# Sums of weight blocks formed in device memory for a seven-product multiply, with the products reordered

## The chip, the core and the metric

The kernel runs on one core of a Trainium2 chip. A core has five engines with an instruction queue each, worked off in order: TensorE (PE: matrix products and transposes, with the weight loads in a row of their own, PEld), VectorE (DVE), ScalarE (ACT), GpSimd (POOL) and SyncE (SP, which here only issues transfers). Engines wait for each other by semaphores. Transfers (DMAs) issued by SP or ACT ("hardware" queues, q1 and q10 in the profile) and by POOL ("software" queue, q0) run on the same 16 DMA engines. Operands of the engines lie in on-chip memory (SBUF), results of PE in accumulator banks (PSUM); weights and inputs lie in device memory (DRAM).

The metric is the device time of one execution in microseconds (us). Before the change: 1409.25 us, the median of 3 runs (1408.93 to 1411.69).

## What is computed

One layer of a hybrid block on 512 tokens of width 1024, everything in float32: a gated delta-rule branch "a" (8 heads) and a retention branch "b" (4 heads), both fed from one projection by `w_in`, gated, projected and mixed, then an MLP. Cut to what matters here:

```python
proj = xn @ w_in                       # 512 x 1024 times 1024 x 14352
qa, ka, va, za, ..., qb, kb, vb, gb, gate_a, gate_b = split(proj)
oa = chunk_gated_delta_rule(conv_silu(qa, ka, va), beta, g)
ya = (rmsnorm(oa) * silu(za)) @ w_br_a
ob = chunk_retention(rotary(qb), rotary(kb), vb)          # vb, gb: 4 heads x 512 columns
yb = (rmsnorm(ob) * silu(gb)) @ w_br_b
mix = (sigmoid(gate_a) * ya + sigmoid(gate_b) * yb) @ w_out
x = x + rmsnorm(mix)
out = x + rmsnorm(square(relu(rmsnorm(x) @ w_up)) @ w_down)
```

The change concerns `vb` and `gb`, the values and the gates of branch b: per head a product of the 512 x 1024 activations with two blocks of 1024 x 512 of `w_in`.

## The kernel before, in words

Every large product is made of three float32r products: operands are split into a high and a low part, and high x high, high x low and low x high are added in PSUM (`mm3`, L78, whose three matmuls are L81, L82 and L83). A weight block of 512 KB is loaded by SP into a tile `raw` (`weights`, L85, the load is on L91), then split: ACT copies the high part `whi` (L104), DVE subtracts to get the low part `wlo` (L105). Pool `ring` holds 2 `raw`, 3 `whi` and 3 `wlo`. A list `raw_pools` says from which pools `weights` takes `raw` in turn: the ring alone, and late in branch b also a tag `ych` with 2 buffers in the pool of that stage (`raw_pools.append`).

Stages in order of time:

- The input is normed, transposed and split into `xs` (tiles `actT`).
- Branch a (pools `pa` and, inside it, `pa2`): `keys`, `base_inverse`, `double_blocks`, `values_queries` and `recurrence` for four groups `g2` of two heads, then for each group `gated` (gate product), `ya_partial` of the group before, and `gated_features` (the group's result transposed, 4 times 4 transposes by PE on L202 through one PSUM bank, each four taken out by ACT on L185 and DVE on L186). In `values_queries` each of six convolutions (`conv_silu`, L378) first has POOL clear three columns of a tile `c_raw` with 2 buffers (L380), ACT fills the rest, DVE runs the taps (L390, L394) and PE transposes the result (`to_tokens`). POOL also masks `at` (`affine_select`, L588) and moves small blocks through DRAM scratch (`scr`, `rn`, `rt`).
- Branch b (pool `pb`, whose tiles take the memory that `pa2` and `pa` leave): `feature_sums` (sums of quarters of the activations, DVE and ACT), then for each head `h`: `scores` (products for q and k, `rotary` on DVE (L824 to L832), score products in PSUM tag `dl`), at h = 0 `ya_partial(3)` and the gate product of branch a, else `branch_partial`; `outputs`, with `values_and_gates` in it, and `gated_features`.
- Mixing, the output product and the MLP.

`values_and_gates` (L738) makes the values and gates of a head by a seven-product scheme (Strassen-Winograd) on 2 x 2 blocks: token halves by row halves of `w_in`, and the two column blocks c1 (values) and c2 (gates). Call the weight blocks w11, w12, w21, w22 (first index the row half, second c1 or c2). Four of the products need sums of weight blocks: w11+w12, w22+w12, w11+w12+w22, and all four. Each product takes two weight tiles of 512 KB (`ks` = 0, 1) and each tile feeds 12 matmuls on L758. Before, these sums are formed in SBUF just in time: class `Sums` (L111) keeps one `raw` tile per `ks` for a running sum ("chain", in tag `ych`): after DVE has split it for one product, POOL issues a transfer that adds the next block onto it (`accum_op=ALU.add`, L124), and it is split again. The order of products is 11, 12, s1, s3, s2, s4, 22.

The instructions are ordered on each engine when the program is built: the tile framework schedules by priorities (`tc.high_priority`), and `tc.keep_in_program_order` pins the matmuls of a product. Waits between tiles are set by it too: a tile of `pb` waits until the last readers and writers of the memory it takes from `pa` and `pa2` are done; and DMAs issued by POOL go through eight semaphore lanes in turn, so that one waits for the eighth before it.

Of the kernel before, what the change touches and what calls it, by code (L numbers as in the profile page):

```python
# [60 lines left out]
def hybrid_block_kernel(ctx: ExitStack, tc: tile.TileContext, a: dict, out: bass.AP):  # L61
# [46 lines left out]
            lo[:, :n].rearrange("p (k c) -> p k c", k=nk),  # L108
        )

    class Sums:  # L111


        def __init__(self, pool, tag, blocks):
            self.raw = pool.tile([P, 1024], F32, tag=tag, name="raw", bufs=2)
            self.blocks, self.n = blocks, 0

        def next(self, more=1):
            for _ in range(more):
                src, k0, c0 = self.blocks[self.n]  # L120
                block = src[k0 * P : (k0 + 2) * P, c0 : c0 + 512].rearrange("(k p) c -> p k c", p=P)
                dst = self.raw.rearrange("p (k c) -> p k c", k=2)
                if self.n:
                    nc.gpsimd.dma_start(dst, block, accum_op=ALU.add)  # L124
                else:
                    nc.sync.dma_start(dst, block)
                self.n += 1
            return split_weights(self.raw, 1024, 2)

    def feature_major(src, xs, c0, ncols, kts, krow0=0):  # L130

# [296 lines left out]
    with tc.tile_pool(name="pa", bufs=1) as pa:  # L428
# [46 lines left out]
        def base_inverse(g4, pool):  # L475
# [32 lines left out]
                nc.gpsimd.dma_start(rt[bs, ns, bs], scr_t[b].rearrange("n (m c) -> m n c", m=32))  # L508
            return scr_r

        def double_blocks(pool, scr_r, m0):

            rn = pool.tile([P, 8, 64], F32, tag="qf", name="rn", bufs=2)
            nc.gpsimd.memset(rn, 0.0)
            for b in range(3):
                bs = slice(32 * b, 32 * b + 32)
                cs = slice(32 * (b % 2), 32 * (b % 2) + 32)
                nc.gpsimd.dma_start(
                    rn[bs, :, cs], scr_r[b, m0 % 16 : m0 % 16 + 8].rearrange("n (m c) -> m n c", m=32)
                )  # L520
# [24 lines left out]
            nc.vector.tensor_scalar(rn[hi, :, 0:32], p2[hi], -1.0, None, ALU.mult)  # L545
            lo, hi = slice(0, 64), slice(64, 128)
            p3 = bank(64)
            for n in range(8):
                nc.tensor.matmul(p3[hi, n, :], mt[lo, m0 + n, hi], rn[lo, n, :], start=True, stop=True)
            nc.vector.tensor_copy(y[hi], p3[hi])  # L550
            p4 = bank(64)
            for n in range(8):
                nc.tensor.matmul(p4[lo, n, :], y[hi, n, :], rt[hi, m0 + n, hi], start=True, stop=True)
            nc.vector.tensor_scalar(rt[lo, ns, hi], p4[lo], -1.0, None, ALU.mult)

        def values_queries(g2, pool):
# [16 lines left out]
            for hh in range(2):  # L573
# [9 lines left out]
                for c in range(4):  # L583
# [4 lines left out]
            nc.gpsimd.affine_select(  # L588
                at, at, pattern=[[0, 8], [1, P]], compare_op=ALU.is_ge, fill=0.0, base=0, channel_multiplier=-1
            )  # L590

            rq = pool.tile([P, 8], F32, tag="rq", name="rq", bufs=2)
            nc.vector.tensor_scalar(ssq, ssq, EPS, None, ALU.add)
# [81 lines left out]
        def gated(g2, rows, pool):  # L675
            pss = token_major(w_in, x_tile, OFF_ZA + g2 * 512, 8)
            zz = pool.tile([P, 4, T], F32, tag="zz", name="zz")
            gate_rows(pss, rows, lambda t: zz[:, t, :])

        with tc.tile_pool(name="pa2", bufs=1) as pa2:  # L680
            keys(0, pa2)
            scr = base_inverse(0, pa2)
            vq = values_queries(0, pa2)
            keys(1, pa2)
            double_blocks(pa2, scr, 0)
            og = None
            for g2 in range(4):
                rows = recurrence(g2, vq, pa2)
                if g2 == 0:
                    double_blocks(pa2, scr, 8)  # L690
                    scr = base_inverse(1, pa2)
                if g2 < 3:
                    vq = values_queries(g2 + 1, pa2)
                if g2 == 1:
                    double_blocks(pa2, scr, 16)
                    double_blocks(pa2, scr, 24)
                gated(g2, rows, pa2)
                if g2:
                    ya_partial(g2 - 1, og)
                og = gated_features(rows, lambda f: na[:, f % 2 : f % 2 + 1])  # L700
# [3 lines left out]
    with tc.tile_pool(name="pb", bufs=1) as pb_:  # L704
# [6 lines left out]
        def tmp(name):  # L711
            return pb_.tile([P, T], F32, tag="tm", name=name, bufs=8)
# [20 lines left out]
                nc.vector.tensor_tensor(s[:, 1], a, s[:, 0], ALU.subtract)  # L733
                quarters[f"s{i + 1}"] = [s[:, 0], s[:, 1]]

        feature_sums()

        def values_and_gates(c1, c2, g, out1, out2):  # L738

            def rows(kh, ks):  # L740
                return 4 * kh + 2 * ks

            chain = [
                Sums(pb_, "ych", [(w_in, rows(0, ks), c1), (w_in, rows(0, ks), c2),
                                  (w_in, rows(1, ks), c2), (w_in, rows(1, ks), c1)])
                for ks in range(2)
            ]

            def product(pss, x, ks, wts, first):
                wh, wl = wts  # L750
# [17 lines left out]
            def bank():  # L768
                return [psm.tile([P, T], F32, tag="mm", name="mm") for _ in range(2)]

            def one(kh, c, ks):
                return Sums(ring, "raw", [(w_in, rows(kh, ks), c)]).next()

            def two(ks):
                return Sums(ring, "raw", [(w_in, rows(1, ks), c2), (w_in, rows(0, ks), c2)]).next(2)

            a = bank()
            for ks in range(2):
                product(a, "11", ks, chain[ks].next(), True)
            p1 = [tmp("p1") for _ in range(2)]  # L780
            with tc.high_priority(400):
                for t in range(2):
                    nc.scalar.copy(p1[t], a[t])
            for ks in range(2):
                product(a, "12", ks, one(1, c1, ks), False)
            for t in range(2):
                out1(t, a[t])
            c = bank()
            for ks in range(2):
                product(c, "s1", ks, chain[ks].next(), True)  # L790
# [4 lines left out]
            for ks in range(2):  # L795
                product(b, "s3", ks, two(ks), True)
# [4 lines left out]
            for ks in range(2):  # L801
                product(b, "s2", ks, chain[ks].next(), False)
            u3s = [tmp("u3") for _ in range(2)]
            with tc.high_priority(400):
                for t in range(2):
                    nc.vector.tensor_tensor(u3s[t], p1[t], b[t], ALU.add)
            for t, u3 in enumerate(u3s):
                nc.vector.tensor_tensor(p7[t], u3, p7[t], ALU.subtract)
                nc.vector.tensor_tensor(g[:, 2 + t, :], g[:, 2 + t, :], u3, ALU.subtract)
                out2(2 + t)  # L810
            for ks in range(2):
                product(c, "s4", ks, one(1, c2, ks), False)
# [3 lines left out]
            for ks in range(2):  # L816
                product(b, "22", ks, chain[ks].next(), False)
            for t in range(2):
                nc.vector.tensor_tensor(p1[t], p1[t], b[t], ALU.add)
                out1(2 + t, p1[t])  # L820

        def rotary(pss, dst):
            r = [tmp("ro") for _ in range(4)]
# [39 lines left out]
        def outputs(h, scs):  # L863
# [13 lines left out]
            values_and_gates(OFF_VB + h * 512, OFF_GB + h * 512, gs, value, gate)  # L877
# [266 lines left out]
```

## Time and profile before

| what | value |
| --- | --- |
| median of three runs | 1409.25 us (1408.93 to 1411.69) |
| the profiled execution: its own time | 1408.78 us |
| its span in the trace | 1407.1 us |
| PEld busy | 1124.0 us (80%) |
| DVE, ACT, POOL busy | 869.7 us (62%), 611.2 us (43%), 93.4 us (7%) |
| mean granted TensorE clock | 0.993 |
| read from DRAM / written | 143.81 MB / 5.77 MB, 106 GB/s over the span |
| values and gates of the four heads (first and last start on L758) | 587.1 to 921.7 us |

The trace lists the instructions of one execution with their start, their duration and what ended the idle time before them. Matmuls are pipelined: one of 512 columns lasts 0.39 us in the records while the next starts 0.227 us after it, so that a gap under about 0.16 us doesn't show as idle PE; the weight loads (PEld) show it. "PEclk" is the clock granted to TensorE as a share of full speed. A view by windows gives the busy time of each engine in a stretch, the clock, the mean share of the 16 DMA engines and what they moved.

### The profile page before, as it was taken

The numbers are of one execution on the slowest core, as the hardware profiler recorded it, in microseconds if no ns is written. First come the engines' busy times: TensorE is split into PE (matmuls) and PEld (weight loads), VectorE is DVE, ScalarE is ACT, GpSimd is POOL, SyncE is SP. The second block draws the span as 40 slices with busy tenths as digits, with TensorE's granted clock in tenths as the row PEclk, the third lists the DMA queues.
The fourth block names the chain that finished last, engine by engine and source line by source line (L and its number), as shares of the span: only waits on it lengthen the run. The fifth ranks groups of instructions, "written<-read, shape, count | busy, mean of one in ns | idle before, by whom it ended". The sixth has DMA issues, their size and how long they took to land.

```text
span 1407.1 us, 17528 instructions
## 1 busy us (share of the span) xinstructions
PE 1377.1 (98%) x6670; PEld 1124.0 (80%) x6670; DVE 869.7 (62%) x1539; ACT 611.2 (43%) x1134; POOL 93.4 (7%) x136
## 2 busy tenths in 40 slices
PE   8999999999999989999999999999999999999997
PEld 5888787878888878877878778778888888888886
DVE  5599889944755594467378486565785334344445
ACT  6778564725534232343453443443354333232331
POOL 1112300200000000110200200200000000000000
PEclk9999999999999999999999999999999999999999
DMA  5232412221321333682672753851724232323321
GB/s 158 75 93 74 118 31 75 71 78 46 90 90 45 104 115 97 166 208 75 120 187 82 151 150 76 184 174 61 229 99 137 92 103 90 105 90 105 105 75 61
DMA packets 79223, 150.72 MB, mean 107 GB/s; under 512 B 5183, under 2 KB 18641, under 8 KB 78626
## 3 DMA queue, kind: packets, MB, share of 16 engines
q1 hardware_dynamic: 66128, 119.03, 27.4%
q0 software_dynamic: 12288, 29.32, 10.2%
q8 instruction: 52, 0.85, 0.2%
q10 hardware_dynamic: 722, 1.25, 0.2%
q14 instruction: 33, 0.27, 0.1%
HBM read 143.81 MB, written 5.77 MB: 106 GB/s over the span
## 4 chain that ended last, share of the span: by engine, by line
PE 79%; DVE 9%; DMA 6%; ACT 3%; issue 2%; POOL 0%; SPq 0%; DVEq 0%; POOLq 0%; ACTq 0%
PE mm L81 21%; PE mm L82 21%; PE mm L83 21%; DMA raw<-in_w_in_dram 5%; PE mm L758 4%; DVE wlo L105 3%; PE tr L202 2%; ACT whi L104 2%; DVE c_y L390 1%; PE dl L621 1%; PE dl L649 1%; PE dl L82 1%; PE dl L81 1%; PE dl L83 1%; PE dl L613 1%
## 5 line engine op out<-in xcount | busy, mean ns | idle before, releaser
L105 DVE TENSOR_TENSOR wlo<-raw,whi 128x1024 fp32r<-128x1024 f32 x232 | 283.6, 1223 | 357.3 <-ACT whi L104 356.0
L104 ACT CAST whi<-raw 128x1024 fp32r<-128x1024 f32 x232 | 243.9, 1052 | 473.4 <-PE mm L82 239.3
L82 PE MATMUL mm<-actT,whi 128*128 128x512 f32 (+1 forms) x528 | 209.2, 396 | 1.2 <-DVE actT L236 1.2
L81 PE MATMUL mm<-actT,whi 128*128 128x512 f32 (+1 forms) x528 | 206.5, 392 | 1.0 <-ACT actT L235 1.0
L83 PE MATMUL mm<-actT,wlo 128*128 128x512 f32 (+1 forms) x528 | 207.1, 393 | 0.0
L81 PEld LDWEIGHTS mm<-actT,whi 128*128 128x128 f32 x528 | 99.7, 189 | 21.6 <-ACT actT L235 1.4
L82 PEld LDWEIGHTS mm<-actT,whi 128*128 128x128 f32 x528 | 100.3, 190 | 20.3 <-DVE actT L236 1.4
L83 PEld LDWEIGHTS mm<-actT,wlo 128*128 128x128 f32 x528 | 100.1, 190 | 18.4
L81 PE MATMUL mm<-hn,whi 128*128 128x512 f32 (+1 forms) x288 | 105.6, 367 | 0.5 <-DVE r L1067 0.5
L82 PE MATMUL mm<-hn,whi 128*128 128x512 f32 (+1 forms) x288 | 105.4, 366 | 0.0
L81 PE MATMUL mm<-og,whi 128*128 128x512 f32 x256 | 100.9, 394 | 4.3 <-DVE ro L825 4.3
L83 PE MATMUL mm<-hn,wlo 128*128 128x512 f32 (+1 forms) x288 | 105.1, 366 | 0.0
L83 PE MATMUL mm<-og,wlo 128*128 128x512 f32 x256 | 100.6, 393 | 0.0
L82 PE MATMUL mm<-og,whi 128*128 128x512 f32 x256 | 100.6, 393 | 0.0
L81 PE MATMUL mm<-whi,actT 128*128 128x512 f32 x216 | 86.2, 399 | 0.1
L82 PE MATMUL mm<-wlo,actT 128*128 128x512 f32 x216 | 85.8, 397 | 0.0
L83 PE MATMUL mm<-whi,actT 128*128 128x512 f32 x216 | 85.5, 397 | 0.0
L758 PE MATMUL mm<-whi,xsum 128*128 128x512 f32 x256 | 82.3, 397 | 2.0 <-ACT whi L104 2.0
L390 DVE SCALAR_TENSOR_TENSOR c_y<-c_raw,convw,c_y 128x512 f32<-128x512 f32 x96 | 70.5, 752 | 3.4 <-ACT c_y L388 2.8
L81 PEld LDWEIGHTS mm<-hn,whi 128*128 128x128 f32 x288 | 54.3, 188 | 10.1 <-DVE r L1067 0.8
L83 PEld LDWEIGHTS mm<-hn,wlo 128*128 128x128 f32 x288 | 54.2, 189 | 8.8
L82 PEld LDWEIGHTS mm<-hn,whi 128*128 128x128 f32 x288 | 54.3, 189 | 8.7
(314 smaller groups left out, 2468.2 us busy)
## 6 DMA issues: line engine op xcount, KB each, us to landing
raw<-in_w_in_dram SPq DMA_DIRECT2D x113, 512.0 KB, 3.8
raw<-in_w_up_dram SPq DMA_DIRECT2D x36, 512.0 KB, 3.8
raw<-in_w_in_dram POOLq DMA_DIRECT2D x32, 512.0 KB, 7.0
raw<-in_w_down_dram SPq DMA_DIRECT2D x32, 512.0 KB, 3.7
raw<-in_w_br_a_dram SPq DMA_DIRECT2D x16, 512.0 KB, 3.7
raw<-in_w_br_b_dram SPq DMA_DIRECT2D x16, 512.0 KB, 3.7
raw<-in_w_out_dram SPq DMA_DIRECT2D x8, 512.0 KB, 3.9
x<-in_x_dram SPq DMA_DIRECT2D x4, 512.0 KB, 6.1
```

Of the source, the lines that this page charges most:

```text
L81: nc.tensor.matmul(ps, lh, rh, start=first, stop=False)
L82: nc.tensor.matmul(ps, lh, rl, start=False, stop=False)
L83: nc.tensor.matmul(ps, ll, rh, start=False, stop=last)
L104: nc.scalar.copy(hi[:, :n], raw[:, :n])
L105: nc.vector.tensor_tensor(lo[:, :n], raw[:, :n], hi[:, :n], ALU.subtract)
L202: nc.tensor.transpose(ps, src, ident)
L390: nc.vector.scalar_tensor_tensor(y, raw[:, j : j + T], tap(j), y, ALU.mult, ALU.add)
L613: nc.tensor.matmul(ks[:, hh, :], kf[:, h0 + hh, cs], state[:, hh, :], start=True, stop=True)
L621: nc.tensor.matmul(px[:, hh, :], rt[:, nn[hh], :], vx[:, hh, :], start=True, stop=True)
L649: nc.tensor.matmul(po[:, hh, :], at[:, 4 * hh + c, :], vn[:, hh, :], start=True, stop=True)
L758: m = nc.tensor.matmul(pss[t], lhs[i // 2], rhs[i % 2], start=first and k + i == 0, stop=k + i == 5, skip_group_check=not first,)
```

## The change

- `Sums` is gone. A new class `BlockSums` allocates four tiles of 1 MB in DRAM per head. On construction POOL issues four transfers DRAM to DRAM that fill them with w11, w11, w22 and w21. `add(i)` issues two accumulating transfers of 512 KB, DRAM onto DRAM, for one tile. The results: t0 = w11+w12, t1 = w11+w12+w22, t2 = w22+w12, t3 = all four.
- `vg_pair(h0)` does this for two heads: 8 copies and 16 accumulating transfers on POOL's queue. It is called in branch a for g2 = 1 (heads 0 and 1) and g2 = 2 (heads 2 and 3), each under `tc.issue_after` the last entry of `pool_marks`: the last `rn` load of `double_blocks`, or the mask of `values_queries`.
- `values_and_gates` loads every weight tile by SP: six of 512 KB from `w_in` and eight from the sums, per head. Its order of products is 11, 12, s1, s3, s2, 22, s4; product 22 has two PSUM banks of tag `dl` of its own.
- The tag `ych` joins `raw_pools` at the start of branch b: all weight loads of that branch go in turn to 2 + 2 `raw` buffers. `feature_sums` is called after `scores(0)`.

```diff
-    class Sums:
-        def __init__(self, pool, tag, blocks):
-            self.raw = pool.tile([P, 1024], F32, tag=tag, name="raw", bufs=2)
...
+    class BlockSums:
+        def __init__(self, src, c1, c2, tag):
+            def block(kh, c):
+                return src[4 * kh * P : 4 * (kh + 1) * P, c : c + 512].rearrange("(k p) c -> p k c", p=P)
+            self.w12, self.first = block(0, c2), [block(0, c1), block(0, c1), block(1, c2), block(1, c1)]
+            self.t = [dr.tile([P, 4, 512], F32, tag=f"{tag}{i}", name="sums", bufs=1) for i in range(4)]
+            for t, b in zip(self.t, self.first):
+                nc.gpsimd.dma_start(t, b)
+        def add(self, i):
+            src = (self.w12, self.t[2], self.w12, self.t[1])[i]
+            for k in range(0, 4, 2):
+                nc.gpsimd.dma_start(self.t[i][:, k : k + 2, :], src[:, k : k + 2, :], accum_op=ALU.add)
+        def weights(self, i, ks):
+            return block_weights(self.t[i - 1][:, 2 * ks : 2 * ks + 2, :])
+    def block_weights(block):
+        n = next(loads)
+        pool, tag = raw_pools[n % len(raw_pools)]
+        raw = pool.tile([P, 1024], F32, tag=tag, name="raw", bufs=2)
+        nc.sync.dma_start(raw.rearrange("p (k c) -> p k c", k=2), block)
+        return split_weights(raw, 1024, 2)
...
+            pool_marks.append(mark)
...
+            vg_sums = []
+            def vg_pair(h0):
+                pair = [BlockSums(w_in, OFF_VB + h * 512, OFF_GB + h * 512, f"vg{h}") for h in range(h0, h0 + 2)]
+                for i in (2, 0, 1, 3):
+                    for sums in pair:
+                        sums.add(i)
+                return pair
             for g2 in range(4):
                 rows = recurrence(g2, vq, pa2)
...
+                if g2 in (1, 2):
+                    with tc.issue_after(pool_marks[-1].ins):
+                        vg_sums += vg_pair(2 * g2 - 2)
                 gated(g2, rows, pa2)
...
-        feature_sums()
-        def values_and_gates(c1, c2, g, out1, out2):
+        def values_and_gates(sums, c1, c2, g, out1, out2):
...
-            for ks in range(2):
-                product(b, "s2", ks, chain[ks].next(), False)
+            multiply(b, "s2", total(2), False)
...
+            d = [psx.tile([P, T], F32, tag="dl", name="dl", bufs=3) for _ in range(2)]
+            multiply(d, "22", total(4), True)
+            for t in range(2):
+                nc.vector.tensor_tensor(p1[t], p1[t], d[t], ALU.add)
+                out1(2 + t, p1[t])
+            multiply(c, "s4", plain(1, c2), False)
             for t in range(2):
                 nc.vector.tensor_tensor(g[:, t, :], c[t], p7[t], ALU.subtract)
                 out2(t)
-            for ks in range(2):
-                product(b, "22", ks, chain[ks].next(), False)
...
+        raw_pools.append((pb_, "ych"))
         for h in range(4):
             scs = scores(h)
             if h == 0:
+                feature_sums()
                 ya_partial(3, prev)
...
-        raw_pools.append((pb_, "ych"))
         gates = []
```

More of the change, by code (lines that the diff above doesn't have):

```diff
@@ L109, in split_weights @@
         )
-    class Sums:
-        def __init__(self, pool, tag, blocks):
-            self.raw = pool.tile([P, 1024], F32, tag=tag, name="raw", bufs=2)
[L116 to L128, printed above, removed]
+    class BlockSums:
[18 more added lines that the diff above has]
+        return split_weights(raw, 1024, 2)
     def feature_major(src, xs, c0, ncols, kts, krow0=0):
@@ L587, in values_queries @@
                     )
-            nc.gpsimd.affine_select(
+            mask = nc.gpsimd.affine_select(
                 at, at, pattern=[[0, 8], [1, P]], compare_op=ALU.is_ge, fill=0.0, base=0, channel_multiplier=-1
             )
+            pool_marks.append(mask)
             rq = pool.tile([P, 8], F32, tag="rq", name="rq", bufs=2)
@@ L734, in feature_sums @@
                 quarters[f"s{i + 1}"] = [s[:, 0], s[:, 1]]
-        feature_sums()
-        def values_and_gates(c1, c2, g, out1, out2):
[L740 to L747, printed above, removed]
+        def values_and_gates(sums, c1, c2, g, out1, out2):
             def product(pss, x, ks, wts, first):
@@ L769, in bank, with plain, multiply, total @@
                 return [psm.tile([P, T], F32, tag="mm", name="mm") for _ in range(2)]
[L771 to L775, printed above, removed]
+            def plain(kh, c):
+                return lambda ks: weights(w_in, 4 * kh + 2 * ks, 2, c, 512)
+            def multiply(pss, x, wts, first):
+                for ks in range(2):
+                    product(pss, x, ks, wts(ks), first)
+            def total(i):
+                return lambda ks: sums.weights(i, ks)
             a = bank()
-            for ks in range(2):
-                product(a, "11", ks, chain[ks].next(), True)
+            multiply(a, "11", plain(0, c1), True)
             p1 = [tmp("p1") for _ in range(2)]
@@ L783, in values_and_gates @@
                     nc.scalar.copy(p1[t], a[t])
-            for ks in range(2):
-                product(a, "12", ks, one(1, c1, ks), False)
+            multiply(a, "12", plain(1, c1), False)
             for t in range(2):
@@ L788, in values_and_gates @@
             c = bank()
-            for ks in range(2):
-                product(c, "s1", ks, chain[ks].next(), True)
+            multiply(c, "s1", total(1), True)
             with tc.high_priority(400):
@@ L794, in values_and_gates @@
             b = bank()
-            for ks in range(2):
-                product(b, "s3", ks, two(ks), True)
+            multiply(b, "s3", total(3), True)
             p7 = [tmp("p7") for _ in range(2)]
@@ L800, in values_and_gates @@
                     nc.scalar.copy(p7[t], b[t])
-            for ks in range(2):
-                product(b, "s2", ks, chain[ks].next(), False)
[L803 to L809, printed above, removed]
-                out2(2 + t)
-            for ks in range(2):
-                product(c, "s4", ks, one(1, c2, ks), False)
+            multiply(b, "s2", total(2), False)
+            for t in range(2):
+                nc.vector.tensor_tensor(p1[t], p1[t], b[t], ALU.add)
+                nc.vector.tensor_tensor(p7[t], p1[t], p7[t], ALU.subtract)
+                nc.vector.tensor_tensor(g[:, 2 + t, :], g[:, 2 + t, :], p1[t], ALU.subtract)
+                out2(2 + t)
+            d = [psx.tile([P, T], F32, tag="dl", name="dl", bufs=3) for _ in range(2)]
+            multiply(d, "22", total(4), True)
+            for t in range(2):
+                nc.vector.tensor_tensor(p1[t], p1[t], d[t], ALU.add)
+                out1(2 + t, p1[t])
+            multiply(c, "s4", plain(1, c2), False)
             for t in range(2):
```

9 lines of the change are left out of this document (3 added, 6 removed).

## The prediction, as put on record before the result

> **What bounds the kernel now.** I read the page first, then who waited for whom on PE's weight loads in 480 to 940 us (branch b and its entry), then the timelines of POOL, SP and PE where the change puts work.
>
> ```profile
> span 1407.1 us, 17528 instructions
> PE 1377.1 (98%) x6670; PEld 1124.0 (80%) x6670; DVE 869.7 (62%) x1539; ACT 611.2 (43%) x1134; POOL 93.4 (7%) x136
> ```
>
> PE sets the time, and a change that leaves its matmuls as they are can only fill or open gaps in it. The waits of the weight loads show the gaps (columns: total us, times, longest), PE's own rows the longest one:
>
> ```profile
> PEld mm L758 <- DVE wlo L105: 5.4, 6, 1.1
> ...
> PEld dl L82 <- DVE vr L869: 2.3, 4, 0.9
> PEld dl L81 <- ACT vr L868: 1.8, 1, 1.8
> ...
> PEld mm L758 <- ACT whi L104: 3.7, 4, 1.4
> ```
> ```profile
> 510.75 0.39 PE L83 MATMUL mm<-actT,wlo 128*128 128x512 f32 x1
> 515.48 0.77 PE L81 MATMUL mm<-og,whi 128*128 128x512 f32 x1 [4.34 <-DVE ro L825]
> ```
>
> So the just-in-time sums cost 5.4 + 3.7 = 9.1 us over four heads, values that come late for the outputs 4.1 us, and one wait at branch b's entry 4.3 us, where `feature_sums` keeps DVE from the rotary. After some of them the granted clock falls. In these windows the columns are length, busy us of PE, PEld, DVE, ACT and POOL, then clock, DMA share and GB/s:
>
> ```profile
> 514.00:516.00 2.00, 0.52 (x1) 0.50 (x2) 2.00 (x4) 0.00 (x0) 0.00 (x0) 0.53 0.65 146
> 516.00:518.00 2.00, 2.00 (x6) 1.56 (x5) 2.00 (x4) 0.84 (x2) 0.00 (x0) 0.50 0.30 116
> 518.00:520.00 2.00, 2.00 (x6) 1.52 (x6) 2.00 (x4) 0.38 (x1) 0.00 (x0) 0.50 0.00 0
> 520.00:522.00 2.00, 2.00 (x8) 1.60 (x7) 2.00 (x5) 0.04 (x1) 0.00 (x0) 0.76 0.00 0
> ```
> ```profile
> 602.00:604.00 2.00, 2.00 (x10) 1.38 (x8) 1.11 (x1) 1.34 (x2) 0.00 (x0) 1.00 1.13 206
> ...
> 610.00:612.00 2.00, 2.00 (x7) 1.52 (x6) 1.85 (x2) 1.63 (x2) 0.62 (x1) 0.50 0.86 245
> 612.00:614.00 2.00, 2.00 (x8) 1.63 (x7) 0.46 (x1) 0.38 (x1) 1.73 (x2) 0.72 0.50 64
> ```
>
> The missing clock costs 0.25 + 1.0 + 1.0 + 0.5 = 2.7 us after the entry wait and 1.0 + 0.6 = 1.6 us after head 0's wait. The row at 602 also shows accumulating transfers with the DMA engines full: 206 GB/s.
>
> **The change part by part.**
>
> *Products from prepared sums: -9 us.* Gone are 32 accumulates in branch b and the waits for them. Each head now makes 14 plain loads, one per 12 matmuls (12 x 0.227 = 2.7 us). One buffer's round is landing, whi and wlo:
>
> ```profile
> raw<-in_w_in_dram SPq DMA_DIRECT2D x113, 512.0 KB, 3.8
> ...
> raw<-in_w_in_dram POOLq DMA_DIRECT2D x32, 512.0 KB, 7.0
> ```
> ```profile
> L105 DVE TENSOR_TENSOR wlo<-raw,whi 128x1024 fp32r<-128x1024 f32 x232 | 283.6, 1223 | 357.3 <-ACT whi L104 356.0
> L104 ACT CAST whi<-raw 128x1024 fp32r<-128x1024 f32 x232 | 243.9, 1052 | 473.4 <-PE mm L82 239.3
> ```
>
> 3.8 + 1.05 + 1.22 = 6.1 us; four buffers give a tile each 1.5 us, where two would give 3.0 and fall behind. So most of the 9.1 + 1.6 us goes; I take 9 and leave 1.7 for splits that queue behind other work. Matmuls, splits and the additions of the results keep their number. The other loads of branch b gain nothing from four buffers: the list of waits names none of them.
>
> *Product 22 before s4: -3.5 us.* The last values are made while s4 runs (24 x 0.227 = 5.4 us), so most of the 4.1 us of `vr` goes; the gates, now last, are needed only after the outputs. The two `dl` banks were last used a `branch_partial` earlier: no cost.
>
> *Entry of branch b: +8 us.* With `ych` in the list from the start, the first and third of the four q and k weight loads of `scores(0)` go to memory that `pa2` still holds. In the built order the first waits for the last transpose of branch a's last `gated_features` (L202), and PE, which before ran q matmuls between these transposes, has nothing between the sixteen:
>
> ```
> before: ya_partial, 4 tr, 11 q, 4 tr, 8 q, 4 tr, 8 q, 4 tr, 69 q and k, ya_partial ...
> after:  ya_partial, 16 tr, 96 q and k, 18 ya_partial, 24 score products ...
> ```
> ```profile
> 487.23 0.60 PE L202 MATMUL tr<-cmat,vt 128*128 128x128 f32 x4
> ...
> 490.22 0.66 PE L202 MATMUL tr<-cmat,vt 128*128 128x128 f32 x4
> ...
> 492.57 0.60 PE L202 MATMUL tr<-cmat,vt 128*128 128x128 f32 x4
> ```
>
> Four transposes share one bank, and their round is 492.57 - 490.22 = 2.35 us. The fourth starts at 487.2 + 3 x 2.35 = 494.3 and is done at 494.9; load 3.8, whi 1.05: q starts at 499.8. 96 matmuls are 21.8 us, waiting for the first wlo 0.7: k ends at 522.3. Before, it ended at 511.0, and PE went on at 515.5. `feature_sums` now finds DVE idle during PE's wait, so the 4.3 us go, but 522.3 - 515.5 = 6.8 us are lost net. The score products then wait for k's rotary: DVE, ACT and DVE take about 6 us after k, 18 matmuls cover 4.1: some 1.5 us more. The clock's 2.7 us stay, as a wait as long stands there. If the cover existed (first loads to the ring), this part would be a gain of 4 to 7 us.
>
> *Forming the sums: +20 us.* POOL's queue, in order, gets 24 transfers after the last `rn` load of `double_blocks`, and 24 after the mask:
>
> ```profile
> 285.00 1.73 POOL L518 DMA_DIRECT2D rn<-scr  x3 [0.29 <-POOL rn L514]
> 369.06 0.10 POOL L380 MEMSET c_raw<- 128x3 f32 x1 [82.32 <-DVE c_y L394]
> ...
> 391.16 1.10 POOL L588 TENSOR_SCALAR_AFFINE_SELECT at<-at 128x1024 f32<-128x1024 f32 x1 [12.07 <-DVE ssq L593]
> ```
> ```profile
> 496.14 0.59 POOL L706 DMA_DIRECT2D rope<-in_c_rope_dram  x1 [103.87 <-PE tr L202]
> ```
> ```profile
> 370.55 0.75 DVE L390 SCALAR_TENSOR_TENSOR c_y<-c_raw,convw,c_y 128x512 f32<-128x512 f32 x1
> ```
>
> Behind the first batch stand four clears of `c_raw` and the mask. The first clear is used by DVE's taps at 370.55; behind these stand DVE's splits and PE's transposes. So the batch has 370.6 - 286.7 = 84 us. POOL is free once its last transfer is issued; that one reads t1 as the 20th transfer leaves it, so 8 copies and 12 accumulates must have landed.
>
> No copy DRAM to DRAM is in the trace. Lower bound of one: the rate of SP's queue, 119.03 MB in 27.4% of 1407.1 us = 309 GB/s, 3.4 us per 1 MB. Upper: read and write one after the other, 6.8. An accumulate: 0.524 MB at 206 GB/s = 2.5 us, upper 2.5 + 1.7 for writing to DRAM.
>
> ```profile
> q1 hardware_dynamic: 66128, 119.03, 27.4%
> ```
> ```profile
> 287.00:371.00 84.00, 83.68 (x466) 67.48 (x466) 41.99 (x74) 35.70 (x66) 0.20 (x2) 1.00 0.24 68
> 392.00:496.00 104.00, 104.00 (x474) 85.26 (x474) 58.36 (x104) 36.07 (x62) 0.26 (x1) 1.00 0.26 81
> ```
>
> Weights take 0.24 of the engines there. Low: (8 x 3.4 + 12 x 2.5) / 0.76 = 75, with 4 us for the first issue and last landing 79: hidden. High: (54 + 50) / 0.76 + 4 = 141: 57 us late. The accumulate row already reads two streams and writes one at 206 GB/s, so reading and writing do overlap; I take a third of the way up: 4.6 and 3.1 us, (37 + 37) / 0.76 + 4 = 101 us, 17 us late, and 3 for the clock after such a stall. POOL's own part is less:
>
> ```profile
> L124 POOL DMA_DIRECT2D raw<-in_w_in_dram x32: 1172/1182/1675, 579.1 to 906.5; - x32
> ```
>
> 256 rows take 1.18 us, so 8 copies of 512 rows some 19 us, under the transfers. The trace has no copy to go by, and the Trainium skill gives a price: "DMA: Bandwidth & Descriptors", section "Latency and other measured facts", has copies between tensors in device memory at 207 to 214 GB/s at best. By that a copy is an estimated 5.1 us, and the sum would be 5 us more; no run here shows it yet.
>
> The second batch starts 20 us late, at 412, and takes 74 / 0.74 + 4 = 104 us, to 516. Next in the queue is `rope`, which PE's last transpose releases at about 515: no cost at this price, and no slack left.
>
> Sum, against the execution's 1408.8 us: - 9 - 3.5 + 8 + 20 = 1424 us. The execution lies 0.5 us under the median, which I leave.
>
> **The rivals.**
>
> *The batch is hidden (not slower).* Place: POOL's queue from 287 to 371 us. If copies and accumulates cost what the nearest rows say, it ends in 79 of its 84 us; the point is a sum of 61 us for 8 copies and 12 accumulates. For it: an accumulate is already three streams. Against: no row has both ends in DRAM. Time: 1408.8 - 12.5 + 8 = 1404 us, 1402 with the whole gain.
>
> *The batches collide with the entry.* At 5.7 and 3.6 us: (46 + 43) / 0.76 + 4 = 121, 37 us late and 3 for the clock. The second runs from 432 to 556, and `rope` lands behind its last four accumulates (4 x 3.6 / 0.74 = 19 us) at 575, where the rotary wants it at 499.8 + 40 + 15 = 555: 20 us more. Time: 1404 + 40 + 20 = 1464 us. At the upper bounds it passes 1500.
>
> *Weight loads fall behind beside the batch.* In dense stretches a tile is used each 24 x 0.227 = 5.45 us; two buffers allow 10.9 us a round, less 2.3 for the splits and 0.4 for the issue: 8.2 us to land.
>
> ```profile
> DMA to landing us min/median/max: 3.5/3.7/10.5
> ```
>
> At 10.5 us each load loses 1.15 us; 27 loads fall into the two batches: 31 us at most, 15 as a mean, 1419 us if nothing else is late. Against: landings near 8 us are hidden. The Trainium skill's page "DMA: Bandwidth & Descriptors", section "Queues, rings and completion order", says that an engine takes turns between queues, a packet each; by it a load would land in some 7 us (an estimate), and this rival falls; the trace has no stretch with both queues full for long.
>
> *The products gain nothing*, the splits being late and not the sums: 1404 + 12.5 = 1417 us. Against: the waits named end with transfers of 7.0 us where plain ones take 3.8.
>
> **How the numbers follow.** Batch late by 5 to 35 us: 0.45 (1409 to 1444 us). Hidden: 0.25. Collision: 0.18. Loads: 0.07. No gain: 0.05. About 0.2% is what a measurement of this kernel tells from no change. Faster (under 1406.4): 0.22, the hidden batch without its upper edge. Same: 0.08, that edge and the lowest of the first case. Slower: 0.70. The range 1402 to 1466 holds all but the upper half of the collision and a few hundredths below.
>
> **What would show it.** In the profile after: POOL's first clear of `c_raw` behind the batch later than 371 us, PE waiting there for DVE's convolution, and the clock at half after it. If the clear is on time, the forecast is wrong and the hidden batch right. At the entry sixteen transposes with gaps and q waiting for a load. In the heads' products, no waits on L758 for splits. Landing times of SP's loads in the batches decide on the loads, the start of `rope` on the collision.

## The result and the profile after

The changed kernel takes 1419.95 us (median of 6 runs, 1416.56 to 1422.03) beside 1409.09 us (6 runs) for the kernel before on the same chip: a ratio of 1.0074, 95% interval 1.0055 to 1.0092, so 10.9 us slower. The profiled execution took 1422.0 us, 2.1 us above that median, while the one of before lies 0.3 us under its own; so the shifts read from the two traces below add up to 13.2 us and not to 10.9. Lines moved by nine and more: L202 is now L211, L380 L389, L588 L600, L624 L637, L758 L772, L825 L834.

The page after, its span, its busy times and its two large DMA queues:

```profile
span 1420.3 us, 17580 instructions
...
PE 1376.5 (97%) x6670; PEld 1127.5 (79%) x6670; DVE 869.8 (61%) x1539; ACT 613.2 (43%) x1134; POOL 98.9 (7%) x152
...
q1 hardware_dynamic: 68560, 131.61, 29.6%
q0 software_dynamic: 14592, 46.10, 12.6%
```

PE works as long as before (1377.1 us then), so the 13.2 us of span are gaps. DVE and ACT, too, are busy as long as before to within 2 us (869.7 and 611.2 us then): the new traffic doesn't slow the engines' own work, it makes them wait. POOL's timeline after shows the first batch and what stands behind it in its queue:

```profile
286.26 1.73 POOL L529 DMA_DIRECT2D rn<-scr  x3 [0.29 <-POOL rn L525]
287.99 5.90 POOL L121 DMA_DIRECT2D sums<-in_w_in_dram  x8
...
359.50 0.81 POOL L127 DMA_DIRECT2D sums<-sums  x1 [2.04 <-DMA sums<-sums]
379.40 0.10 POOL L389 MEMSET c_raw<- 128x3 f32 x1 [19.09 <-DVE c_y L403]
...
401.51 1.10 POOL L600 TENSOR_SCALAR_AFFINE_SELECT at<-at 128x1024 f32<-128x1024 f32 x1 [12.07 <-DVE ssq L606]
...
473.35 0.81 POOL L127 DMA_DIRECT2D sums<-sums  x1 [2.67 <-DMA sums<-sums]
513.65 0.59 POOL L731 DMA_DIRECT2D rope<-in_c_rope_dram  x1 [39.48 <-PE tr L211]
```

POOL is through with the batch at 360.3 us, 72.3 us after its first copy. Then it sits idle for 19.09 us until DVE lets go of `c_raw`: the clear is 10.3 us later than before (379.40 against 369.06), but POOL waits for the others and not they for POOL. The same holds for the mask (12.07 us for DVE's `ssq`) and for `rope`, which waits for PE's transposes.

What is late, PE's weight loads in 286 to 500 us tell. `vn` is a result of the recurrence and `c_y` the first tap of a convolution, both taken out of PSUM by ACT (an "eviction"); `zz` is the gate, taken out by ACT and finished by DVE. The first row is from before, the others from after; before, there were no rows of `zz` and of `c_y` on ACT, and that of `c_y` on DVE had 0.5 us:

```profile
PEld dl L629 <- ACT vn L624: 1.2, 4, 0.3
```
```profile
PEld dl L642 <- ACT vn L637: 7.6, 4, 3.6
PEld mm L81 <- DVE zz L362: 4.8, 5, 2.1
PEld mm L81 <- ACT c_y L397: 3.3, 1, 3.3
...
PEld tr L211 <- DVE c_y L403: 1.5, 1, 1.5
```

That is 6.4 + 4.8 + 3.3 + 1.0 = 15.5 us more than before. ACT makes `vn` and `c_y`, and its own waits in the same stretch have two rows that the kernel before has not:

```profile
ACT whi L104 <- DMA raw<-in_w_in_dram: 36.9, 7, 10.7
...
ACT whi L104 <- DMA raw<-in_w_br_a_dram: 23.0, 5, 7.6
```

The transfers issued in these 214 us, with their median time to landing at the end of the row; before, both kinds of weight load had 3.7 us:

```profile
raw<-in_w_in_dram SPq DMA_DIRECT2D x16, 512.0 KB, 9.3
...
raw<-in_w_br_a_dram SPq DMA_DIRECT2D x10, 512.0 KB, 10.0
```

And ACT's timeline around the longest of these waits shows how a late load becomes a gap of PE, whose row stands below it:

```profile
359.32 1.05 ACT L104 CAST whi<-raw 128x1024 fp32r<-128x1024 f32 x1 [3.73 <-PE mm L82]
371.08 1.04 ACT L104 CAST whi<-raw 128x1024 fp32r<-128x1024 f32 x1 [10.70 <-DMA raw<-in_w_in_dram]
372.03 0.58 ACT L392 COPY c_raw<-mm 128x512 f32<-128x512 f32 x1
372.51 0.69 ACT L397 ACTIVATE c_y<-mm,convw 128x512 f32<-128x512 f32 x1
```
```profile
373.25 0.80 PE L81 MATMUL mm<-actT,whi 128*128 128x512 f32 x1 [2.86 <-ACT c_y L397]
```

ACT takes its instructions in order. A cast whose weights have not landed stands at its head for 10.7 us, with the two evictions of the convolution behind it; PE has no free bank and waits for an eviction, though the weights that it needs next are not the ones that are late: these were cast at 359.32. The load that the cast at 371.08 waited for took 14.5 us to land. PE's other large gaps have the same form: on ACT, the `vn` at 333 and 442 us stand behind casts that waited 2.76 and 5.75 us for their loads, the `zz` at 479 and 485 us behind casts that waited 7.59 and 3.79 us.

Followed from one milestone to the next (before, after): the last `rn` load 285.00, 286.26, a shift that was there before the first new transfer; the first clear +10.3; the first transposes of the last `gated_features` 487.23, 505.07 (+17.8); the first product of head 0 587.1, 611.4 (+24.3); the end +13.2. So the first batch cost 9.1 us (to the clear), the second 7.5, the entry of branch b 6.5, and the products gave 11.1 back (13.2 - 24.3).

The entry in PE's own rows:

```profile
505.07 0.60 PE L211 MATMUL tr<-cmat,vt 128*128 128x128 f32 x4
507.24 0.66 PE L211 MATMUL tr<-cmat,vt 128*128 128x128 f32 x4 [1.57 <-DVE og L195]
509.46 0.82 PE L211 MATMUL tr<-cmat,vt 128*128 128x128 f32 x4 [1.56 <-DVE og L195]
511.85 1.12 PE L211 MATMUL tr<-cmat,vt 128*128 128x128 f32 x4 [1.57 <-DVE og L195]
518.02 0.80 PE L81 MATMUL mm<-actT,whi 128*128 128x512 f32 x1 [5.06 <-ACT whi L104]
```

Sixteen transposes with nothing between them, then 5.06 us for the first q weights. In the heads' products, on the other hand, all matmuls of L772 last 389 ns, and the weight loads' waits from 545 to 1000 us are down to three rows; those on L758 for splits (9.1 us) and those for `vr` (4.1 us), the values converted for the outputs, are gone:

```profile
PEld tr L211 <- DVE o L907: 4.2, 8, 0.8
PEld dl L81 <- ACT osq L901: 0.9, 4, 0.2
PEld dl L83 <- DVE kr L841: 0.3, 2, 0.2
```

### The profile page after: what moved, and what is told of

Read it like the earlier page. It is cut to its first block, busy times and chain, and to the rows that moved or that the text cites. A ratio compares the mean times of both kernels' runs of the same rounds, so it can differ in the third digit from the quotient of the medians.

```text
span 1420.3 us, 17580 instructions
## 1 busy us (share of the span) xinstructions
PE 1376.5 (97%) x6670; PEld 1127.5 (79%) x6670; DVE 869.8 (61%) x1539; ACT 613.2 (43%) x1134; POOL 98.9 (7%) x152
## 4 chain that ended last, share of the span: by engine, by line
PE 80%; DVE 8%; DMA 8%; ACT 3%; issue 1%; SPq 0%; DVEq 0%; POOL 0%; ACTq 0%
PE mm L81 19%; PE mm L83 19%; PE mm L82 19%; PE mm L772 9%; DMA raw<-in_w_in_dram 5%; PE tr L211 2%; DVE wlo L105 2%; DMA raw<-in_w_br_a_dram 2%; PE dl L772 2%; ACT whi L104 1%; DVE c_y L399 1%; PE dl L81 1%; PE dl L83 1%; PE dl L82 1%; PE dl L662 1%
## 5 line engine op out<-in xcount | busy, mean ns | idle before, releaser
L81 PEld LDWEIGHTS mm<-actT,whi 128*128 128x128 f32 x528 | 101.3, 192 | 29.9 <-ACT whi L104 5.5
L82 PEld LDWEIGHTS mm<-actT,whi 128*128 128x128 f32 x528 | 101.6, 192 | 20.7 <-DVE actT L245 1.3
L772 PE MATMUL mm<-whi,xsum 128*128 128x512 f32 x256 | 80.1, 389 | 0.0
L81 PEld LDWEIGHTS mm<-hn,whi 128*128 128x128 f32 x288 | 54.3, 188 | 10.2 <-DVE r L1077 0.8
```

Source lines behind the costliest of these rows:

```text
L81: nc.tensor.matmul(ps, lh, rh, start=first, stop=False)
L82: nc.tensor.matmul(ps, lh, rl, start=False, stop=False)
L772: m = nc.tensor.matmul(pss[t], lhs[i // 2], rhs[i % 2], start=first and k + i == 0, stop=k + i == 5, skip_group_check=not first,)
```

## The experiments

Two theories stood first. *POOL's queue* is the prediction's: the clears of `c_raw` stand behind the batch. *Late loads* is its third rival: SP's weight loads land late beside the batch, and their casts hold up ACT. Each ratio is over runs of the kernel before on the same chip, as the record gives it; it is not the quotient of the medians shown.

**No forming at all** (`e1_no_forming`). The eight sum tiles of a head are plain blocks of `w_in`, so values and gates are those of other weights.

```
-            self.t = [dr.tile([P, 4, 512], F32, ...) for i in range(4)]
-            for t, b in zip(self.t, self.first):
-                nc.gpsimd.dma_start(t, b)
+            self.blocks = [block(0, c1), block(0, c1), block(1, c2), block(1, c1)]
...
-            return block_weights(self.t[i - 1][:, 2 * ks : 2 * ks + 2, :])
+            return block_weights(self.blocks[i - 1][:, 2 * ks : 2 * ks + 2, :])
```

> The transfers that form the sums are left out; the eight tiles per head are loaded from blocks of w_in of the same size, so values and gates are wrong. From the first rn load behind which a batch stands to the last transposes of branch a, the trace after is 16.6 us longer than the one before (9.1 by the mask, 7.5 more by the transposes). If the batches cause this, by whatever way, the time falls by 15 to 17 us to 1403 to 1405 us. If something else of the new order does, it stays near 1420.

Measured: 1402.16 us, ratio 0.9933 (0.9918 to 0.9948). The 48 transfers cost 17.8 us, near the 16.6 of the milestones (17.7 beside the next kernel, which ran on the same chip and takes as long as the change). PE's wait for `vn` is back at 1.2 us, and the entry's 5.0 us for the first q weights stay. This sizes the cost and doesn't yet say which theory is right.

**The clears on DVE** (`e2_clears_on_dve`), which takes POOL's queue out of the convolution:

```
-        nc.gpsimd.memset(raw[:, 0:3], 0.0)
+        nc.vector.memset(raw[:, 0:3], 0.0)
```

> The clears of c_raw go to DVE's queue, all 32; nothing else is changed. Theory POOL (the prediction's): the batches make POOL late for the clears, so the time falls by 9 us or more, to 1411 us or less. Theory loads: POOL was free at 360 us and the clear waited for DVE, the loss is in weight loads that land in 9 to 14 us beside the batches; the time stays at 1420 us, give or take 2, and the loads land as late as before.

Measured: 1419.88 us, ratio 1.0055 (1.0036 to 1.0073), no different from the change. Its waits have the same rows, 7.2 us for `vn`. The theory of POOL's queue falls.

**Copies alone** (`e6_copies_only`) and **more copies** (`e8_more_copies`). The first leaves the accumulates out, the second puts six copies a head in their place, so that a batch is 20 copies long; in both, each sum holds a plain block of weights.

```
-            for k in range(0, 4, 2):
-                nc.gpsimd.dma_start(self.t[i][:, k : k + 2, :], src[:, k : k + 2, :], accum_op=ALU.add)
+            return
```
```
+            for _ in range(2 if i in (1, 3) else 1):
+                nc.gpsimd.dma_start(self.t[i], self.first[i])
```

> The change without its 32 accumulates in device memory: only the 16 copies of 1 MB are issued, so sums 1 to 4 hold a plain block of weights each, and values and gates are those of other weights. The loads theory has the loss follow the time in which loads run beside the batch: the copies take about half of each batch (some 36 of 72 us), so 7 to 10 of the 16.6 us come back, 1409 to 1413 us. If only the accumulates delay the loads, all come back, 1402; if only the copies do, 1419.

> The change with its accumulates replaced by more copies of 1 MB, so that each batch is copies alone and lasts about as long as the change's (20 copies, some 70 us at 3.5 us each); sums 1 to 4 hold a plain block each, values and gates are those of other weights. It tells two readings of e6_copies_only apart. If it is the place that counts (the copies of the change end before the recurrence starts, and only what runs beside the recurrence and the convolutions delays their evictions), the loss returns: 1412 to 1420 us. If accumulates are what delays loads or engines, and copies do not, 1401 to 1405.

Measured: copies alone 1402.91 us (0.9942, 0.992 to 0.9964), so nearly the whole loss is gone and not half of it: the proportional forecast missed. By the expectation this spoke for accumulates alone, or else for the place, since the copies end before the recurrence starts; the second kernel was made to tell these apart. More copies: 1411.89 us (1.0015, 0.9996 to 1.0033), just under the band of the one reading and well over that of the other. Copies delay loads too: these are the weight loads issued from 286 to 325 us with copies alone (9.7 and 10.2 us in the change),

```profile
raw<-in_w_in_dram SPq DMA_DIRECT2D x4, 512.0 KB, 6.6
raw<-in_w_br_a_dram SPq DMA_DIRECT2D x2, 512.0 KB, 10.4
```

and PE waits for none of them. There it works on a gate product and a partial product, whose evictions have time. With more copies, traffic lasts into the recurrence, and the waits for `vn` return (286 to 500 us of that kernel):

```profile
PEld dl L642 <- ACT vn L637: 6.9, 4, 3.2
...
PEld mm L81 <- DVE zz L362: 1.2, 1, 1.2
```

So lateness is free where nothing that PE needs soon stands behind a cast, and dear beside the recurrence and the convolutions. The 8 us between this kernel and the change are mostly `zz` and `c_y`: the one is 1.2 us here and not 4.8, the other (3.3) did not come back. Whether accumulates press harder than copies, or the last six transfers only fell otherwise, stays open. The traces lean to the first: the load issued between 350 and 360 us, the one behind PE's long wait above, landed in 14.5 us beside the accumulates of the change and in 6.6 us beside these copies.

**Casts without a head start** (`e7_casts_late`): the casts and remainders of the weights that are loaded in groups 1 and 2 of the delta rule lose their scheduling priority.

```
     def split_weights(raw, n, nk, keep=None, ahead=200):
+        if late[0]:
+            ahead = 0
...
             for g2 in range(4):
+                late[0] = g2 in (1, 2)
```

> The change, but the casts and remainders of the weights loaded while the groups 1 and 2 of the delta rule run no longer get their head start of 200 in the scheduler, so they stand later in ACT's and VectorE's orders. Loads theory: a load that is late then holds up fewer of vn and c_y, and 5 to 12 us of the 16.6 come back, 1408 to 1415, unless the casts come late for PE by themselves: then PE waits for whi and wlo where it waited for vn and c_y, and the time is 1418 or more. It does not say what the lateness costs where the load is needed at once.

Measured: 1422.97 us, ratio 1.0079 (1.0054 to 1.0104); a miss. The wait for `vn` grew:

```profile
PEld dl L646 <- ACT vn L641: 10.3, 4, 6.3
PEld tr L215 <- DVE c_y L407: 3.1, 1, 3.1
PEld mm L81 <- DVE zz L366: 2.4, 1, 2.4
```

The order on each engine is fixed when the program is built, and without the head start the casts did not come behind the right evictions. This setting of the priority, at least, is no remedy.

**The entry** (`e5_ring_first`, `e9_entry`, and on the kernel before `b1_sums_later`, `b2_sums_last`). In e5 the two `ych` buffers join the list after the first scores; e9 also has `feature_sums` after the partial product. b1 moves `feature_sums` of the kernel before to where the change has it, b2 behind the partial product. Shown is the edit of e9:

```
-        raw_pools.append((pb_, "ych"))
         for h in range(4):
             scs = scores(h)
             if h == 0:
-                feature_sums()
+                raw_pools.append((pb_, "ych"))
                 ya_partial(3, prev)
+                feature_sums()
```

> The tag ych joins the list after scores(0) and not before it, so that the first q and k loads go to the ring. If the entry's loss comes from loads that wait for the memory of pa2, PE has q matmuls between the transposes again, and the time falls by at least the 6.5 us that the entry lost, and by 13 us where the rotary's wait of before (4.3 us and 2.7 us of clock) is gone too, as feature_sums comes later: 1407 to 1413 us. If DVE's sums are the limit there, 1413 us is the best; if the transposes' round trips are, 1420.

> The kernel before with one edit: feature_sums is called after scores(0). If DVE's sums alone kept PE waiting for the rotary, 4.3 us and 2.7 us of clock go: 1402 us. If the scheduler puts the sums at the same place of DVE's queue or another wait takes their place, 1409 us.

> The change, forming its sums in branch a as it does, with the entry to branch b of c2_ring_first and c3_sums_by_head: branch b's two raw buffers join after the first scores, and the feature sums follow the last partial product of branch a. e5_ring_first had the first of the two alone and gained 3 us, with the wait for acc L435 (4.3 us) left, which the feature sums caused. Theory: that wait goes and 2 to 6 us more come than in e5_ring_first: 1411 to 1415 us. If the wait for acc stays or another as long takes its place, 1416 to 1418.

> The kernel before, with the feature sums after the last partial product of branch a (b1_sums_later had them between the first scores and the partial product, and no gain: the wait for the rotary went, a wait of 4.4 us for acc L426 came). Theory: both waits are gone and 3 to 7 us come: 1402 to 1407 us, and what the best version gains over this one is the work of the products alone. If the first products now wait for the feature sums, 1408 or more.

Measured: e5 1416.91 us (1.0044, 1.0026 to 1.0061), above its band, b1 1410.46 (1.0009, 0.9994 to 1.0025), e9 1409.53 (0.9994, 0.9983 to 1.0005), b2 1404.89 (0.9964, 0.9951 to 0.9978). b1 removed the wait of 4.3 us for the rotary and got this row in its place:

```profile
532.31 0.64 PE L81 MATMUL mm<-og,whi 128*128 128x512 f32 x1 [4.38 <-DVE acc L426]
```

The operations of `feature_sums` now stood ahead of DVE's evictions of the partial product instead of ahead of the rotary. The same wait, 4.3 us for `acc`, stands in e5 and is gone in e9; it kept e5 from its gain. Behind the partial product they hold up nothing: b2 gains 5.0 us on the kernel before, and e9 10.4 us on the change, somewhat more than was expected.

**The sums formed in branch b** (`c1_sums_in_b`, `c2_ring_first`, `c3_sums_by_head`), where loads have four raw buffers. c1 issues one head at a time, behind the decay tables and a write of `ya_d`; c2 adds the entry of e9; c3 puts the batch of head h + 1 behind a clear of `oss` in the outputs of head h. That clear waits until head h - 1 is through with the tile, so the batches of heads 2 and 3 start near the ends of heads 0 and 1:

```
             gs = pb_.tile([P, 4, T], F32, tag="kr", name="gs")
+            ss = pb_.tile([P, 4], F32, tag="oss", name="oss")
+            mark = nc.gpsimd.memset(ss, 0.0)
+            if h < 3:
+                vg_head(h + 1, mark)
```

> The same copies and accumulates as in the change, but issued one head at a time in branch b (head 0 right after its decay table, head 1 after the first write of ya_d, heads 2 and 3 after the decay tables of the heads before), where the weight loads have four raw buffers instead of two; PE's order is that of the change throughout. Loads theory (late loads beside the batch, casts at the head of ACT's queue): with four buffers a load may land later by two more tiles of products before a cast is late, so most of the 16.6 us that the two batches cost in branch a comes back, 1402 to 1408 us, and loads in 500:620 land at 9 us or more without PE waits of more than 2 us in sum; if the traffic itself slows the engines, wherever it runs, 1416 to 1424.

> The kernel with the sums formed in branch b, and with the first q and k loads of branch b on the ring's buffers alone (the two buffers of branch b are appended after the first scores) and the feature sums after the last partial product of branch a instead of before it. If the entry loss is the 16 transposes in a row and the first load that waits for branch a's pool, and the feature sums only stood in the way of the evictions of the partial product, the 6.5 us of the entry come back too: 1395 to 1401 us. If the entry is bound by the rotary on VectorE and by the rope load whatever stands beside it, no more than 3 us below the kernel before it.

> The kernel c2_ring_first with the sums of heads 1 to 3 issued on POOL behind a clear of the next head's oss, which waits for the last reader of the head before: so head 2's and head 3's copies and accumulates run beside the scores and the partial products, not beside the products of the head before, where the cast of a late load stood ahead of the conversion of the values in ACT's order. Loads theory (a late load costs where its cast holds up something that PE needs at once): the PE waits at 627:640 and 735:748 of c2_ring_first, some 12 and 4 us with the clock, go, and new ones stay under 4 us: 1394 to 1401 us. If the batch costs the same wherever it runs, 1409 to 1413 as before.

Measured: c1 1428.48 us (1.0118, 1.0097 to 1.014), slower than the change and a miss; c2 1411.31 (1.0006, 0.9991 to 1.002), above its band, and 17 us under c1 by an edit that gives the change 10.4 (why it gives more here is not shown); c3 1394.06 us (0.9877, 0.9855 to 0.9899), at the lower end of its band and faster than both kernels. Four buffers did not save c1 and c2, since a batch (from 589 us in c1, 588 in c2) fell on head 0's products. By its place in POOL's queue, behind the write of `ya_d`, it is head 1's; head 2's ran before it. ACT in c1:

```profile
648.51 1.04 ACT L104 CAST whi<-raw 128x1024 fp32r<-128x1024 f32 x1 [9.08 <-DMA raw<-in_w_in_dram]
649.46 1.13 ACT L876 CAST vr<-p 128x512 fp32r<-128x512 f32 x2
```

and c2, in windows (length, busy us of PE, PEld, DVE, ACT and POOL, clock, DMA share, GB/s), with c3 below it:

```profile
620.00:640.00 20.00, 12.04 (x43) 8.53 (x41) 11.39 (x16) 7.17 (x11) 3.41 (x5) 0.87 1.09 242
640.00:660.00 20.00, 19.20 (x80) 15.24 (x81) 13.21 (x30) 5.71 (x12) 0.80 (x1) 0.87 0.62 177
```
```profile
620.00:640.00 20.00, 19.37 (x87) 15.54 (x86) 16.30 (x33) 8.56 (x16) 3.07 (x5) 1.00 0.52 161
640.00:660.00 20.00, 20.00 (x97) 16.30 (x95) 16.10 (x23) 7.38 (x11) 5.54 (x5) 1.00 1.03 282
```

It is the cast ahead of the conversion of the values, the mechanism of branch a in another place. c3 starts its third batch at 635 us and not at 588. In its second window the DMA engines are full (1.03) and PE has no gap. c3's page reads

```profile
span 1392.0 us, 17595 instructions
...
PE 1371.3 (99%) x6670; PEld 1124.7 (81%) x6670; DVE 869.5 (62%) x1539; ACT 613.6 (44%) x1134; POOL 99.7 (7%) x156
```

## Why the prediction was right in sign and wrong in its largest step

- **Products from prepared sums, -9, and product 22 before s4, -3.5.** Right. The trace has -11.1 for the two; c3 and b2, which share the place of `feature_sums` and differ mainly in the products once the forming is hidden, stand 10.8 us apart (on two chips whose kernels before differ by 0.4 us). The waits that were to go are the ones that went.
- **Entry of branch b, +8.** Right in mechanism and nearly in size: 6.5 by the milestones, with the 16 transposes and a first q load that waits. The 1.5 us for k's rotary, the rest of the 8, did not come: no row of PE or PEld from 500 to 620 us waits for it. The line that with the first loads on the ring it would be a gain of 4 to 7 us was too short. e5 does that and leaves a loss of 3.5 (6.5 - 3.0), because PE then leaves DVE no idle time for `feature_sums`; with these behind the partial product e9 makes it a gain of 3.9 (10.4 - 6.5).
- **Forming the sums, +20.** The size came out near (16.6 by the milestones, 17.8 by e1), the mechanism did not. The failing step is the price of the transfers, "a third of the way up" between the bounds, and with it the wait of 17 us for POOL's queue: the batch took 72 us and not 101, and fits its 84. What the runs show in its place are PE's waits for evictions behind the casts of late loads, 15.5 us more than before. Both real prices lie at the lower bounds. These windows of the change hold copies (first row) and accumulates (second row), with weight loads beside them:

```profile
300.00:310.00 10.00, 10.00 (x47) 8.24 (x45) 8.57 (x15) 4.40 (x6) 2.40 (x2) 1.00 0.99 354
...
350.00:358.00 8.00, 8.00 (x37) 6.66 (x37) 3.54 (x11) 3.96 (x11) 2.44 (x3) 1.00 1.06 204
```

  1.05 MB at 354 GB/s is 3.0 us for a copy, 0.524 MB at 204 GB/s 2.6 us for an accumulate; the bounds were 3.4 and 2.5. By these prices the prediction's own sum is (24 + 31) / 0.76 + 4 = 77 us.
- **The signs** that were to show this step came, in some form, all three: the first clear later than 371 us, PE waiting for DVE's convolution, the clock at half. Two rows of the change, the clock (0.50, after the gap at 373 us) and PE's wait:

```profile
374.00:376.00 2.00, 2.00 (x7) 1.52 (x6) 1.97 (x4) 1.20 (x2) 0.00 (x0) 0.50 0.73 194
```
```profile
379.40 0.66 PE L211 MATMUL tr<-cmat,c_y 128*128 128x128 f32 x4 [1.07 <-DVE c_y L403]
```

  They don't tell the two theories apart, since anything that delays the convolution delays its clears as well. POOL's idle 19.09 us ahead of the clear does, and so does e2.
- **The rival of the hidden batch** had the length of the batch right and its time, 1404 us, wrong by the loads: e1, where nothing is formed, stands at 1402.
- **The rival of the late loads**, 15 us and 1419 us at a chance of 0.07, is what happened in branch a. It was put aside because landings near 8 us are hidden; they were 9.3 and 10.0 us. Its picture was a steady loss per load; what the runs show is a loss at the few places where a cast stands ahead of `vn`, `c_y` or `zz`. The Trainium skill's page "DMA: Bandwidth & Descriptors", section "Queues, rings and completion order", says that an engine takes turns between queues; the 7 us that the prediction estimated from it are too low here. The measured 9.3 and 10.0 us decide, and by them the rival had stood.
- **The collision with the entry** did not come: the last transfer left POOL at 474.2 us, 39 us before `rope`.
- **No gain from the products** fell with the rows of L758.

So the sum held by luck, for its largest term was explained by the wrong queue: a cost that was not there stood in for one of its size that had been put aside.

## What to carry to other kernels

Transfers that are off the critical path and that nobody waits for still cost time if they fill the DMA engines beside a stream of loads with two buffers; compare the landing time under load with what the buffers tolerate, before any queue. A late load hurts through what stands behind its cast on an in-order engine, so place background transfers where the evictions behind the casts have slack: the same 48 transfers cost 17 us beside the recurrence and left no new gap on PE in c3, where they run beside scores, partial and gate products (its PE waits of 2.2 us for the rotary's `ro` and 1.1 us for `kr` are those of e9). When an operation is moved away from a wait, look at what it now stands ahead of (4.3 us for the rotary became 4.4 us for `acc`).

## What the runs showed of the hardware

Copies with both ends in device memory run faster than expected: 365 to 370 GB/s of copies and loads together from 410 to 440 us of the kernel with more copies,

```profile
410.00:420.00 10.00, 9.18 (x41) 7.27 (x40) 4.72 (x8) 2.60 (x3) 0.70 (x1) 1.00 1.02 370
420.00:430.00 10.00, 10.00 (x46) 8.29 (x45) 3.97 (x6) 1.05 (x1) 0.00 (x0) 1.00 1.02 369
430.00:440.00 10.00, 7.33 (x37) 5.82 (x36) 6.53 (x9) 4.10 (x6) 3.60 (x5) 1.00 1.03 365
```

where seven weight loads were issued from 400 to 440 us (0.092 MB per us), which leaves some 275 GB/s for the copies (an estimate). The Trainium skill's page "DMA: Bandwidth & Descriptors", section "Latency and other measured facts", has 207 to 214 GB/s at best for copies between tensors in device memory, issued from the sync and scalar queues on tiles of 128 rows of 16 KiB; the trace, with rows of 2 KB on POOL's queue, is above it, and the 5 us that the prediction would have added by it were not there. A weight load of 0.5 MB lands in about 10 us beside copies (9.7 and 10.2 us median from 286 to 325 us of the change) and in 10.5 to 14.5 us beside accumulates (three loads issued from 330 to 372 us), against 3.7 us in the kernel before. And POOL's issue of a copy of 512 rows takes 5.90 / 8 = 0.74 us, less than the 1.18 us that the kernel before shows for a transfer of 256 rows into SBUF with accumulation.
